# Low weight products one contraction block behind, and five queue orders fixed, in a hybrid conv/mLSTM decoder block

## The chip, the cores and the metric

The kernel runs on one core of one Trainium2 chip. The metric is the device time of one execution in microseconds (us). The kernel before takes 1734.45 us, the median of three runs (1732.58 to 1735.91).

The engines are called by their short names: PE (TensorE) does the matrix products and transposes, PEld loads its weights, DVE (VectorE) and ACT (ScalarE) work elementwise, POOL (GpSimd) does a little of that, and SP (SyncE) issues most of the DMA loads. Each engine works through its own queue in order; an instruction that waits holds up all that stands behind it on that engine.

## The reference

One block of a decoder on 1024 tokens with 1024 channels, in float32. Cut to what matters:

```python
h = rms_norm(x, norm_mix_g[l]) * (1.0 + sc1) + sh1
proj = jnp.einsum("bsd,de->bse", h, w_in[l]) + b_in[l]
glu_in, qk_in, v, o_pre, if_pre, merge_pre = jnp.split(proj, IN_SPLITS, axis=-1)
a = glu_in[..., :CONV_WIDTH] * jax.nn.sigmoid(glu_in[..., CONV_WIDTH:])
a = causal_depthwise_conv(a, conv_dw_w[l], conv_dw_b[l])          # 31 taps
qk = jax.nn.silu(causal_depthwise_conv(qk_in, qk_conv_w[l], qk_conv_b[l]))   # 4 taps
hm = mlstm_chunkwise(heads(q), heads(k) * (MLSTM_HEAD_DIM ** -0.5), heads(v), gates[...], gates[...])
y = jnp.einsum("bsd,de->bse", g_conv * y_conv + g_mlstm * y_mlstm, w_out[l])
x = x + g1 * y
h = rms_norm(x, norm_ffn_g[l]) * (1.0 + sc2) + sh2
gt, up = jnp.split(jnp.einsum("bsd,df->bsf", h, w_ffn_up[l]), 2, axis=-1)
x = x + g2 * jnp.einsum("bsf,fd->bsd", jax.nn.silu(gt) * up, w_ffn_down[l])
return rms_norm(x, final_norm_g)
```

The mLSTM has four heads of 256 channels; per chunk it forms decayed scores of q and k, multiplies them with v, and carries a state C from chunk to chunk. The feed-forward width is 2816.

## The kernel before

**Products in three parts.** Each float32 operand is split into a high part, rounded to the matmul's type (`hh`, `whi`), and a low part, the rest (`hl`, `wlo`). A product is the sum hi x hi + hi x lo + lo x hi. The high part of a weight is made by a copy on ACT (L148), the low part by a subtraction on DVE (L149). `mm_k` (L154) does one of eight contraction blocks of a 128 x 1024 output: for hi x hi, hi x lo and lo x hi in turn, two matmuls of 512 columns each, which accumulate in one PSUM tile `mm`. There are two such tiles. `block` and `wblock` run `mm_k` over the eight blocks, 48 matmuls in all.

**The order.** The program is written stage by stage, and a scheduler at build time decides the order in each engine's queue by priorities and what is free. `queue_behind(ins, earlier)` (L173) is a hand-made constraint: `ins` stands behind `earlier` in the queue of their engine. It adds no wait between engines.

**Stages.** Until 45 us conditioning and norm. To about 950 us: the GLU columns with the 31-tap convolution (DVE, L388), the projections and the four mLSTM heads, with projection blocks as other work for PE beside the chain of the chunks. Then w_out (L991 to L1010) and the second norm (to 1085), the up projection (`up_run`, to 1482), and the down projection in four groups of feed-forward blocks (to 1734).

**Heads.** For each head `qk_part` runs `qk_tile` four times, k, k, q, q: one `wblock`, an eviction with bias into `qkraw` (L530, ACT; one buffer), the first tap into `cacc` (L533, ACT; two buffers) and three more taps (L535, DVE). For k follow SiLU into `kf` and back into `cacc` (L539, L540), then `kh` (L543) and `kl` (L544). `v_part` makes v with its own weights in two halves (L583 on ACT, L584 on DVE) and 256-column matmuls (L601 to L605). `mlstm` (L647) goes over four chunks of 256 tokens: scores into `pa` (L627 to L629, in `three`), masking on DVE (L659, L660), their split `sch`, `scl` (L663, L664), transposes of `kf` (L674), scaled keys `kwh`, `kwl` (L676, L677), products with v into `pn` and with the state into `pc`, `num` (L697, L698), and for the first three chunks the new state `Cst` (L714), `Ch` (L715, ACT), `Cl` (L716, DVE). After two chunks `num` is normalised (L734) and transposed (L741). The `qk_part` of a head is written behind the `mlstm` of the head before; the scheduler draws it forward.

**Gate weights.** In `v_part` of head 0, L576 and L577 copy the weights of the gates into the tiles that also hold the v weights.

**Up projection.** `up_run` forms seven products per block of a fast 2 x 2 scheme (`product`, L1104, 12 matmuls each) into banks of PSUM: p1 and p5 share an `mm` tile, p2 and p7 the other, p6 is in `pa`, p3 in `pn`, p4 in `pc`. DVE adds combine them (L1136 to L1147).

**Down projection.** For each group and each of eight token blocks t: `act_split` (L1175) loads the activations and splits them (L1179 ACT, L1180 DVE), matmuls L1299 to L1301 sum into `mm`, and DVE adds the sum to x (L1303). For a block of the next group `down_raw` loads 512 KB of weights into `draw` (two buffers) and scales them on DVE (L1162), and `down_split` splits them into `fa` or `fb` (L1171, L1172).

## Time and profile before

| what | value |
|---|---|
| median of three runs | 1734.45 us (1732.58 to 1735.91) |
| the profiled execution | 1735.88 us |
| its span in the profile | 1734.1 us |
| busy, share of the span: DVE | 1249.7 us, 72% |
| busy, share of the span: ACT | 611.7 us, 35% |
| matmuls | 8360 |
| PE busy in 45 to 270 us | 223.49 of 225 us |
| in 270 to 305 us | 32.49 of 35 us |
| in 305 to 975 us | 667.70 of 670 us |
| in 975 to 1085 us | 103.27 of 110 us |
| in 1085 to 1482 us | 396.24 of 397 us |
| in 1482 to 1560 us | 75.96 of 78 us |

A row of the timeline gives start in us, duration in us, engine, line, operation, output <- inputs with their shapes, the number of instructions in a row that are joined in it, and in brackets the idle time before it and what ended that. A row of waits gives engine and line, what was waited for, total us, times, longest us. A row of windows gives the window, its length, then for PE, PEld, DVE, ACT and POOL busy us and instructions, the granted PE clock, the share of DMA time and GB/s.

### The profile page before, as it was taken

How to read it: one execution, taken by the hardware profiler on the slowest of the kernel's cores; microseconds unless marked ns; L12 is line 12 of the kernel's file. 1: busy time of each engine (PE TensorE's matmuls, PEld its weight loads, DVE VectorE, ACT ScalarE, POOL GpSimd, SP SyncE). 2: the span in 40 equal slices, each digit the busy share in tenths (PEclk: the TensorE clock that was granted, in tenths of full speed). 3: DMA queues.
4: the chain of work that ended last, by engine and by line, in shares of the span. 5: the costliest groups of instructions: out<-in, count | busy, mean ns of one | idle time of the engine just before them, and what ended most of it. 6: DMA issues, size and time to landing. Idle time of an engine off the chain costs nothing. (4 is left out here: it accounts for less than half of the span.)

```text
span 1734.1 us, 20875 instructions
## 1 busy us (share of the span) xinstructions
PE 1692.9 (98%) x8360; PEld 1418.6 (82%) x8360; DVE 1249.7 (72%) x1681; ACT 611.7 (35%) x809; POOL 52.7 (3%) x113
## 2 busy tenths in 40 slices
PE   5999999999999999999999998999999999999998
PEld 4788889888988888888888778888888888778887
DVE  6989998997799669446798668766666665685243
ACT  7424335323433253223522386322222222232122
POOL 0000001000001000000000000000000000000000
PEclk9999999999999999999999999999999999999999
DMA  9221120221111112243694743322222222653121
GB/s 320 63 62 49 37 71 28 61 73 49 37 49 61 61 49 61 73 146 98 209 376 167 230 152 104 98 86 85 86 73 75 84 81 96 226 168 101 58 94 52
DMA packets 194711, 179.91 MB, mean 104 GB/s; under 512 B 7463, under 2 KB 166711, under 8 KB 194615
## 3 DMA queue, kind: packets, MB, share of 16 engines
q1 hardware_dynamic: 177367, 146.61, 27.4%
q10 hardware_dynamic: 17248, 31.99, 5.0%
q8 instruction: 65, 1.06, 0.3%
q14 instruction: 31, 0.25, 0.0%
HBM read 146.06 MB, written 32.51 MB: 103 GB/s over the span
## 5 line engine op out<-in xcount | busy, mean ns | idle before, releaser
L388 DVE SCALAR_TENSOR_TENSOR cacc<-a,col,cacc 128x1024 f32<-128x1024 f32 x240 | 306.8, 1286 | 3.9 <-ACT cacc L386 1.4
L158 PE MATMUL mm<-hh,wlo 128*128 128x512 f32 x864 | 271.2, 391 | 1.5 <-DVE wlo L149 1.5
L158 PE MATMUL mm<-hl,whi 128*128 128x512 f32 x864 | 272.5, 392 | 0.0
L158 PE MATMUL mm<-hh,whi 128*128 128x512 f32 x864 | 271.6, 392 | 0.0
L158 PEld LDWEIGHTS mm<-hh,wlo 128*128 128x128 f32 x864 | 160.3, 188 | 33.6 <-DVE wlo L149 2.7
L158 PEld LDWEIGHTS mm<-hl,whi 128*128 128x128 f32 x864 | 161.0, 188 | 32.1 <-issue 0.5
L158 PEld LDWEIGHTS mm<-hh,whi 128*128 128x128 f32 x864 | 160.5, 188 | 31.6
L148 ACT ACTIVATE whi<-wraw 128x1024 fp32r<-128x1024 f32 x61 | 64.7, 1061 | 226.5 <-PE mm L158 171.3
L149 DVE TENSOR_TENSOR wlo<-wraw,whi 128x1024 fp32r<-128x1024 f32 x61 | 74.5, 1222 | 28.7 <-ACT whi L148 25.2
L1114 PE MATMUL mm<-Bh,gh 128*128 128x512 f32 (+1 forms) x192 | 71.5, 375 | 2.9 <-ACT gh L1051 1.5
L1115 PE MATMUL mm<-Bl,gh 128*128 128x512 f32 (+1 forms) x192 | 71.5, 373 | 0.6 <-DVE Bl L1033 0.6
L604 PE MATMUL mm<-wlo,hh 128*128 128x256 f32 x256 | 72.0, 282 | 0.0
L1116 PE MATMUL mm<-Bh,gl 128*128 128x512 f32 (+1 forms) x192 | 71.2, 371 | 0.0
L1303 DVE TENSOR_TENSOR x<-x,mm 128x1024 f32<-128x1024 f32 x24 | 29.3, 1219 | 52.0 <-PE mm L1301 49.6
L1179 ACT ACTIVATE whi<-wraw 128x512 fp32r<-128x512 f32 (+2 forms) x32 | 25.3, 792 | 114.8 <-PE mm L1301 75.8
L535 DVE SCALAR_TENSOR_TENSOR cacc<-qkraw,col,cacc 128x1024 f32<-128x1024 f32 x48 | 61.5, 1282 | 4.9 <-ACT cacc L533 4.5
L603 PE MATMUL mm<-whi,hh 128*128 128x256 f32 x192 | 54.6, 284 | 0.0
L605 PE MATMUL mm<-whi,hl 128*128 128x256 f32 x192 | 54.2, 283 | 0.0
L1299 PE MATMUL mm<-fa,whi 128*128 128x512 f32 x128 | 50.6, 396 | 1.6 <-DVE cu L1142 0.9
L1300 PE MATMUL mm<-fa,wlo 128*128 128x512 f32 x128 | 50.5, 395 | 1.2 <-DVE wlo L1180 1.2
L1301 PE MATMUL mm<-fa,whi 128*128 128x512 f32 x128 | 50.6, 395 | 0.0
L1052 DVE TENSOR_TENSOR ul<-uraw,uh 128x1024 fp32r<-128x1024 f32 x20 | 24.5, 1225 | 35.4 <-ACT uh L1051 35.4
(444 smaller groups left out, 3893.1 us busy)
## 6 DMA issues: line engine op xcount, KB each, us to landing
wraw<-in_w_in_dram SPq DMA_DIRECT2D x64, 512.0 KB
awt<-in_w_ada_dram SPq DMA_DIRECT2D x32, 512.0 KB
graw<-in_w_ffn_up_dram SPq DMA_DIRECT2D x24, 512.0 KB
uraw<-in_w_ffn_up_dram SPq DMA_DIRECT2D x22, 512.0 KB
draw<-in_w_ffn_down_dram SPq DMA_DIRECT2D x22, 512.0 KB
act_d<-cg ACTq DMA_DIRECT2D x38, 256.0 KB
wad<-in_w_ada_dram SPq DMA_DIRECT2D x16, 512.0 KB
wraw<-in_w_out_dram SPq DMA_DIRECT2D x16, 512.0 KB
```

Of the source, the lines that this page charges most:

```text
L148: nc.scalar.activation(hi, raw, AF.Copy)
L149: (eng or nc.vector).tensor_sub(lo, raw, hi.bitcast(F32))
L158: nc.tensor.matmul(flat(acc)[:, a:b], lhs[:, k, :], rhs[k][:, a:b], start=(first and k == 0), stop=(last and k == kt - 1))
L388: nc.vector.scalar_tensor_tensor(acc, a[:, j:j + S], dw_col(j, ct), acc, op0=OP.mult, op1=OP.add)
L535: nc.vector.scalar_tensor_tensor(cv, raw[:, j:j + S], wcol(j), cv, op0=OP.mult, op1=OP.add)
L603: nc.tensor.matmul(o, hh[k][:, ts_], his[k], start=False, stop=False)
L604: nc.tensor.matmul(o[:, 0:256], hh[k][:, ts_], los[k], start=False, stop=False)
L605: nc.tensor.matmul(o, hl[k][:, ts_], his[k], start=False, stop=(k == KT - 1))
L1114: nc.tensor.matmul(o, a, rh, start=(k == 0), stop=False)
L1115: nc.tensor.matmul(o, a, rl, start=False, stop=False)
L1116: nc.tensor.matmul(o, b, rh, start=False, stop=(k == 3))
L1299: nc.tensor.matmul(o, hi[:, i, :], his[i][:, a:b], start=(i == 0), stop=False)
```

## The change

1. `mm_k`: the lo x hi product of contraction block k is issued one block later, behind the high products of block k + 1; the last block issues its own too. The number of matmuls stays.
2. `qk_tile`: the three DVE taps (L535) are queued behind the last `Cl` subtraction that has been written so far, which is that of the third chunk of the head before.
3. `v_part`: the copies L576 and L577 get high priority.
4. `up_run`: for the last feed-forward block, product 3 is queued behind product 7, and product 4 behind product 3.
5. Down projection: the scaling of `draw` (L1162) is queued behind the addition to x (L1303) of the same t.
6. Down projection: `act_split` is issued one token block ahead.

```diff
--- before.py
+++ after.py
@@ -153,10 +153,15 @@
 
     def mm_k(acc, k, kt, w, xh, xl, parts=HALVES):
         hi, lo = w
-        for lhs, rhs, first, last in ((hi, xh, True, False), (hi, xl, False, False), (lo, xh, False, True)):
+        steps = [(hi, xh, k), (hi, xl, k)]
+        if k:
+            steps.append((lo, xh, k - 1))
+        if k == kt - 1:
+            steps.append((lo, xh, k))
+        for i, (lhs, rhs, j) in enumerate(steps):
             for a, b in parts:
-                nc.tensor.matmul(flat(acc)[:, a:b], lhs[:, k, :], rhs[k][:, a:b],
-                                 start=(first and k == 0), stop=(last and k == kt - 1))
+                nc.tensor.matmul(flat(acc)[:, a:b], lhs[:, j, :], rhs[j][:, a:b],
+                                 start=(k == 0 and i == 0), stop=(i == 3))
 
     def block(src, row0, kt, col0, xh, xl, w=None, busy=0):
         if w is None:
@@ -523,6 +528,8 @@
             nc.scalar.activation(t, t, AF.Exp, scale=sgn)
         nc.vector.tensor_scalar(wsc, wsc, 1.0 / 16, None, op0=OP.mult)
 
+    ahead = {}
+
     def qk_tile(col0, conv_i, scale, name):
         acc = yield from wblock(col0)
         raw = hp.tile([128, 3 + S], F32, name="qkraw", tag="qkraw")
@@ -532,7 +539,9 @@
         wcol = lambda j: cols["qk_w"][:, j * 16 + conv_i:j * 16 + conv_i + 1]
         nc.scalar.activation(cv, raw[:, 0:S], AF.Copy, scale=wcol(0))
         for j in range(1, 4):
-            nc.vector.scalar_tensor_tensor(cv, raw[:, j:j + S], wcol(j), cv, op0=OP.mult, op1=OP.add)
+            ins = nc.vector.scalar_tensor_tensor(cv, raw[:, j:j + S], wcol(j), cv, op0=OP.mult, op1=OP.add)
+            if "state" in ahead:
+                queue_behind(ins, ahead["state"])
         bias = cols["qk_b"][:, conv_i:conv_i + 1]
         if name == "k":
             kf = hp.tile([128, 768], F32, name=f"kf{conv_i % 2}")
@@ -573,8 +582,9 @@
             for i, t in enumerate(wide):
                 n = min(3, KT - 3 * i)
                 ks = slice(3 * i, 3 * i + n)
-                nc.vector.tensor_copy(t[:, 0:n, 256:264], wif_raw[:, ks])
-                nc.vector.tensor_sub(t[:, 0:n, 264:272], wif_raw[:, ks], t[:, 0:n, 256:264].bitcast(F32))
+                with tc.high_priority():
+                    nc.vector.tensor_copy(t[:, 0:n, 256:264], wif_raw[:, ks])
+                    nc.vector.tensor_sub(t[:, 0:n, 264:272], wif_raw[:, ks], t[:, 0:n, 256:264].bitcast(F32))
         for kh in range(2):
             raw, hi, lo = (wp.tile([128, KT, 128], dt, name=n, tag=n).rearrange("p (k a) e -> p k (a e)", a=2)
                            if n != "whi" or h else None for n, dt in (("wraw", F32), ("whi", F32R), ("wlo", F32R)))
@@ -713,7 +723,7 @@
                     else:
                         nc.vector.scalar_tensor_tensor(Cn[:, j, :], C[2][:, j, :], dec[:, c, h:h + 1], pc[:, 0:258], op0=OP.mult, op1=OP.add)
                     nc.scalar.activation(Ch[:, j, :], Cn[:, j, :], AF.Copy)
-                    nc.vector.tensor_sub(Cl[:, j, :], Cn[:, j, :], Ch[:, j, :].bitcast(F32))
+                    ahead["state"] = nc.vector.tensor_sub(Cl[:, j, :], Cn[:, j, :], Ch[:, j, :].bitcast(F32))
                 C = (Ch, Cl, Cn)
             if c % 2 == 0:
                 continue
@@ -1101,7 +1111,7 @@
     PART = {1: (0, 0, "B", 0), 2: (0, 4, "B", 1), 3: (2, 4, "D", 0), 4: (1, 4, "T", 3), 5: (1, 0, "T", 0),
             6: (2, 0, "T", 1), 7: (3, 0, "T", 2)}
 
-    def product(w, i, o, cs):
+    def product(w, i, o, cs, behind=None):
         wi, k0, kind, part = PART[i]
         hi, lo = w[wi]
         for k in range(4):
@@ -1111,9 +1121,12 @@
                 th, tl = (Bh, Bl) if kind == "B" else (Th, Tl)
                 rh, rl = th[k][:, part, cs], tl[k][:, part, cs]
             a, b = hi[:, k0 + k, :], lo[:, k0 + k, :]
-            nc.tensor.matmul(o, a, rh, start=(k == 0), stop=False)
+            begin = nc.tensor.matmul(o, a, rh, start=(k == 0), stop=False)
+            if k == 0 and behind:
+                queue_behind(begin, behind)
             nc.tensor.matmul(o, a, rl, start=False, stop=False)
-            nc.tensor.matmul(o, b, rh, start=False, stop=(k == 3))
+            end = nc.tensor.matmul(o, b, rh, start=False, stop=(k == 3))
+        return end
 
     def up_run(f, w, half=None):
         n = 512 if half is None else 256
@@ -1138,12 +1151,12 @@
         nc.vector.tensor_add(u2, s1, p[6])
         product(w, 5, p[5], cs)
         nc.vector.tensor_add(c12, u2, p[5])
-        product(w, 7, p[7], cs)
+        end = product(w, 7, p[7], cs)
         nc.vector.tensor_add(c21, u2, p[7])
         nc.vector.tensor_add(c22, c21, p[5])
-        product(w, 3, p[3], cs)
+        end = product(w, 3, p[3], cs, end if f == FT - 1 else None)
         nc.vector.tensor_add(c12, c12, p[3])
-        product(w, 4, p[4], cs)
+        product(w, 4, p[4], cs, end if f == FT - 1 else None)
         nc.vector.tensor_add(c21, c21, p[4])
         for i in range(2):
             nc.scalar.activation(cg[i], cg[i], AF.Silu)
@@ -1157,9 +1170,11 @@
 
     groups = [4, 4, 6, 8]
 
-    def down_raw(f, raw, row):
+    def down_raw(f, raw, row, earlier=None):
         nc.sync.dma_start(raw, wdn[f * 128:(f + 1) * 128, :])
-        nc.vector.tensor_mul(raw, raw, row)
+        ins = nc.vector.tensor_mul(raw, raw, row)
+        if earlier:
+            queue_behind(ins, earlier)
         return raw
 
     def down_split(gidx, i, raw):
@@ -1288,22 +1303,24 @@
         wd = []
         if gidx == 1:
             nc.sync.dma_start(grow, bass.AP(tensor=final_norm_g.tensor, offset=final_norm_g.offset, ap=[[0, 128], [1, D]]))
+        split = None
         for t in range(8):
-            hi, lo = act_split(f0, nf, t)
+            hi, lo = split or act_split(f0, nf, t)
             if gidx == 0:
                 x1.append(load_x1(t))
             if gidx < 3:
                 p = ps_mm()
+            split = act_split(f0, nf, t + 1) if t < 7 else None
             for o, a, b in (finish(t) if gidx == 3 else sums(flat(p))):
                 for i in range(nf):
                     nc.tensor.matmul(o, hi[:, i, :], his[i][:, a:b], start=(i == 0), stop=False)
                     nc.tensor.matmul(o, lo[:, i, :], his[i][:, a:b], start=False, stop=False)
                     nc.tensor.matmul(o, hi[:, i, :], los[i][:, a:b], start=False, stop=(i == nf - 1))
             if gidx < 3:
-                nc.vector.tensor_add(x1[t], x1[t], flat(p))
+                added = nc.vector.tensor_add(x1[t], x1[t], flat(p))
                 nn = groups[gidx + 1]
                 for i in range(len(wd), min(nn, (t + 1) * PACE)):
-                    wd.append(down_split(gidx + 1, i, down_raw(f0 + nf + i, fp.tile([128, D], F32, name="draw", tag="draw", bufs=2), g2row)))
+                    wd.append(down_split(gidx + 1, i, down_raw(f0 + nf + i, fp.tile([128, D], F32, name="draw", tag="draw", bufs=2), g2row, added)))
         f0 += nf
```

The lines of the changed kernel are shifted: by 5 from L158 on, by 7 at L530 to L535, by 9 or 10 in the rest of the heads and in w_out, by 13 to 17 in the down projection.

**DVE at the border of heads 0 and 1.** `cacc_2084` is the first k block of head 1, `cacc_2160` the second, `cacc_2237` the first q block, `wlo_2341` the second half of its v weights; `Cl_1849` is head 0's last state before the change and `Cl_1847` after. Before, from the second k block's taps on (those of `cacc_2084` stand 21 rows further ahead):

```order
L535 SCALAR_TENSOR_TENSOR cacc_2160<-qkraw_2157,col2_528,cacc_2160 128x1024 x2
L584 TENSOR_TENSOR wlo_2341<-wraw_2339,whi_2340 128x1024
L698 TENSOR_TENSOR num4_1772<-num4_1772,pn_1817 128x258
L535 SCALAR_TENSOR_TENSOR cacc_2160<-qkraw_2157,col2_528,cacc_2160 128x1024
L677 SCALAR_TENSOR_TENSOR kwl_1762<-pa_1763,wsc_691,kwh_1761 128x256
L699 BN_STATS st4_1773<-num4_1772 128x6
L700 BN_AGGR mv4_1774<-st4_1773 128x2
L714 SCALAR_TENSOR_TENSOR Cst_1498<-Cst_1498,dec_696,pc_1850 128x258
L714 SCALAR_TENSOR_TENSOR Cst_1498<-Cst_1498,dec_696,pc_1860 128x258
L716 TENSOR_TENSOR Cl_1849<-Cst_1498,Ch_1848 128x258
```

After, from the same state on:

```order
L669 TENSOR_TENSOR dms_1335<-dms_1335,pa_1868 128x256
L726 TENSOR_TENSOR Cl_1847<-Cst_1496,Ch_1846 128x258
L670 TENSOR_TENSOR dms_1335<-dms_1335,pa_1868 128x128
L542 SCALAR_TENSOR_TENSOR cacc_2084<-qkraw_2081,col2_528,cacc_2084 128x1024
L674 TENSOR_TENSOR scl_1884<-dms_1335,sch_1883 128x384
L542 SCALAR_TENSOR_TENSOR cacc_2084<-qkraw_2081,col2_528,cacc_2084 128x1024
L708 TENSOR_TENSOR num4_1770<-num4_1770,pn_1917 128x258
L542 SCALAR_TENSOR_TENSOR cacc_2084<-qkraw_2081,col2_528,cacc_2084 128x1024
```

Before, the taps of the second k block stand ahead of the second `kwl` and of the state. After, the taps of both k blocks and of the first q block stand behind the state, and so does `wlo_2341`, 22 rows further on, behind two taps of `cacc_2237`.

**PE at the same place.** `mm_2253` is the second q block of head 1, `mm_2345` its first v tile; `kf`, `kwl`, `sch`, `scl` belong to head 0's third and fourth chunk. Before, within the third chunk:

```order
L628 MATMUL pn_1789<-vl_702,sch_1735 128x258
L158 MATMUL mm_2253<-hh5_87,wlo_2250 128x512
L158 MATMUL mm_2253<-hh6_88,whi_2249 128x512 x2
L629 MATMUL pn_1789<-vh_701,scl_1736 128x258
L158 MATMUL mm_2253<-hl6_475,whi_2249 128x512 x2
L158 MATMUL mm_2253<-hh6_88,wlo_2250 128x512 x2
L158 MATMUL mm_2253<-hh7_89,whi_2249 128x512 x2
L158 MATMUL mm_2253<-hl7_476,whi_2249 128x512 x2
L158 MATMUL mm_2253<-hh7_89,wlo_2250 128x512 x2
L627 MATMUL pc_1850<-vh_701,kwh_1761 128x258
```

After, at the end of the fourth chunk:

```order
L637 MATMUL pn_1945<-vh_701,sch_1883 128x258
L638 MATMUL pn_1945<-vl_702,sch_1883 128x258
L639 MATMUL pn_1945<-vh_701,scl_1884 128x258
L163 MATMUL mm_2253<-hh0_82,whi_2249 128x512 x2
L163 MATMUL mm_2253<-hl0_308,whi_2249 128x512 x2
L163 MATMUL mm_2253<-hh1_83,whi_2249 128x512 x2
L163 MATMUL mm_2253<-hl1_309,whi_2249 128x512 x2
L163 MATMUL mm_2253<-hh0_82,wlo_2250 128x512 x2
```

Before, the q block's matmuls stand between those of the third chunk. After, all 48 stand behind the last score product of the fourth chunk, and the v tile behind them.

**SP in w_out.** `wraw_7753` is the fifth load of w_out, `graw` and `uraw` are the first weights of the up projection, `g1row` the row of gains. Before:

```order
L996 DMA wraw_7753<-in_w_out_dram 128x2x512
L945 DMA g1row_7600<-mrow_d0_7546 128x1024
L1047 DMA graw_7765<-in_w_ffn_up_dram 128x8x128
L1047 DMA uraw_7767<-in_w_ffn_up_dram 128x8x128
L996 DMA wraw_7804<-in_w_out_dram 128x2x512
L996 DMA wraw_7851<-in_w_out_dram 128x2x512
```

After:

```order
L955 DMA g1row_7600<-mrow_d0_7546 128x1024
L1057 DMA graw_7765<-in_w_ffn_up_dram 128x8x128
L1057 DMA uraw_7767<-in_w_ffn_up_dram 128x8x128
L1006 DMA wraw_7753<-in_w_out_dram 128x2x512
L1006 DMA wraw_7804<-in_w_out_dram 128x2x512
L1006 DMA wraw_7851<-in_w_out_dram 128x2x512
```

The load `wraw_7753` has moved from ahead of `g1row`, `graw_7765` and `uraw_7767` to behind them. No edit names it; it follows from the scheduler.

## The prediction

> **What bounds the kernel now.** I read the first part of the page, then TensorE's waits (the bound engine's), then the rows around each wait that the change touches, and the windows where the clock fell.
>
> ```profile
> PE 1692.9 (98%) x8360; PEld 1418.6 (82%) x8360; DVE 1249.7 (72%) x1681; ACT 611.7 (35%) x809; POOL 52.7 (3%) x113
> ```
>
> TensorE (PE) is busy for 1692.9 of 1734.1 us, and the change takes no matmul away. So time can only come from its idle time and from stretches at a lower clock, and any idle time that is added is paid in full. The rows of the waits that the edits touch (us in total, times, longest):
>
> ```profile
> PE pc L629 <- DVE kwl L677: 1.8, 1, 1.8
> PE mm L158 <- DVE wlo L149: 1.5, 2, 0.8
> PE pa L1003 <- ACT whi L997: 1.5, 1, 1.5
> ...
> PE mm L1300 <- DVE wlo L1180: 1.2, 1, 1.2
> ...
> PE mm L1299 <- DVE cu L1142: 0.9, 1, 0.9
> ...
> PE mm L1299 <- DVE x L1303: 0.8, 1, 0.8
> ...
> PE mm L603 <- DVE t L577: 0.6, 1, 0.6
> ```
>
> Without the L1003 row, which no edit aims at, they come to 6.8 us. Two of these waits are followed by a lower granted clock (first column the window, the last three the clock, the DMA share and GB/s):
>
> ```profile
> 270.00:273.00 3.00, 1.24 (x7) 1.03 (x8) 2.88 (x6) 1.00 (x2) 0.10 (x1) 0.91 0.42 92
> 273.00:276.00 3.00, 3.00 (x16) 3.00 (x16) 1.52 (x4) 2.97 (x6) 0.00 (x0) 0.52 0.27 82
> ...
> 1546.00:1550.00 4.00, 4.00 (x12) 3.14 (x12) 3.87 (x5) 2.64 (x3) 0.00 (x0) 0.62 0.40 135
> ```
>
> At clock 0.52 three us do the work of 1.56: 1.4 us lost, and 0.3 in the window before. The 4 us at 0.62 lose 1.5. So the kwl wait costs 1.8 + 1.7 = 3.5 us, with the 0.3 us wait for kwh just before it 3.8; the two waits in the down projection cost 1.2 + 0.8 + 1.5 = 3.5 us.
>
> **The change part by part.** *Low products one block behind (mm_k).* The rows around one of the two wlo waits:
>
> ```profile
> 483.17 0.40 PE L158 MATMUL mm<-hl,whi 128*128 128x512 f32 x1
> 484.31 0.74 PE L158 MATMUL mm<-hh,wlo 128*128 128x512 f32 x2 [0.74 <-DVE wlo L149]
> 484.89 0.40 PE L158 MATMUL mm<-hh,whi 128*128 128x512 f32 x1
> ...
> 262.62 0.62 PE L158 MATMUL mm<-hh,wlo 128*128 128x512 f32 x2
> 263.07 0.62 PE L158 MATMUL mm<-hh,whi 128*128 128x512 f32 x2
> ```
>
> Two matmuls take 0.45 us from start to start, so one takes 0.23. From 483.17 to 484.31 is 1.14 instead of 0.23, and the pair behind takes 0.58 instead of 0.45: 1.0 us lost, and as much at the other place. The first low product now stands behind eight matmuls instead of four: 4 x 0.23 = 0.9 us of cover against waits of 0.8 and 0.7. Both go: -2.0 us. Were the cover short by 0.2, the rest would still be waited for. The number of matmuls stays.
>
> *Copies of the gate weights at high priority.* VectorE's (DVE's) queue holds the same instructions in the same order up to well behind these copies, so the 0.6 us wait at L603 stays: 0.
>
> *Last up block.* The two products that now come last (p3 into pn, p4 into pc) are 24 matmuls, 5.5 us of cover behind p5 and p7, whose reading DVE adds made the first down matmul wait 0.9 us. That bank is free long before: -0.9 us.
>
> *Down projection.* What made x and wlo late (DVE):
>
> ```profile
> 1539.38 1.23 DVE L1162 TENSOR_TENSOR draw<-draw,g2row 128x1024 f32<-128x1024 f32 x1 [1.28 <-DMA draw<-in_w_ffn_down_dram]
> ...
> 1541.65 1.22 DVE L1303 TENSOR_TENSOR x<-x,mm 128x1024 f32<-128x1024 f32 x1
> 1542.79 1.22 DVE L1172 TENSOR_TENSOR fb<-draw,fb 128x1024 fp32r<-128x1024 f32 x1
> 1543.92 0.69 DVE L1180 TENSOR_TENSOR wlo<-wraw,whi 128x512 fp32r<-128x512 f32 x1
> ```
>
> DVE stood 1.3 us waiting for a draw load, with the add of x queued behind. Now the add goes first and the split of the next block is issued one block early. For a block of group 1 DVE has 1.2 + 1.2 + 0.7 + 1.2 = 4.3 us to do (from these rows), while TensorE computes 24 matmuls of 0.23 = 5.5 us. So both waits and their clock go: -3.5 us. What is queued behind the new wait (the scaling of draw behind the add) is fa or fb of the next group and the next wlo. In group 0 and at the border of groups 2 and 3 the sum comes close to 5.5 us: 0 to +1 us, I take +0.5.
>
> *Heads.* This is the large term. Before, the four-tap convolution of the first k block of head 1 ran during head 0's second chunk, so the next block could be evicted early:
>
> ```profile
> 237.71 1.29 DVE L535 SCALAR_TENSOR_TENSOR cacc<-qkraw,col,cacc 128x1024 f32<-128x1024 f32 x1
> ...
> 242.22 1.10 ACT L530 ACTIVATE qkraw<-mm,col 128x1024 f32<-128x1024 f32 x1
> ```
>
> That freed a PSUM bank for the last q block, and its 48 matmuls and the v part filled TensorE's waits in head 0's last two chunks. Now these taps stand behind head 0's last state. TensorE's queue after the change has no block matmul between the k transposes of the third chunk and the last score product of the fourth; the q block comes behind them. Its bank waits for a chain with these steps (DVE, then ScalarE, ACT):
>
> ```profile
> 260.43 0.56 DVE L664 TENSOR_TENSOR scl<-dms,sch 128x384 fp32r<-128x384 f32 x1
> ...
> 271.88 0.48 DVE L677 SCALAR_TENSOR_TENSOR kwl<-pa,wsc,kwh 128x256 fp32r<-128x256 f32 x1
> ...
> 276.12 0.28 DVE L660 TENSOR_TENSOR dms<-dms,pa 128x128 f32<-128x128 f32 x1
> ...
> 279.52 2.60 DVE L535 SCALAR_TENSOR_TENSOR cacc<-qkraw,col,cacc 128x1024 f32<-128x1024 f32 x2
> 282.05 0.42 DVE L698 TENSOR_TENSOR num<-num,pn 128x258 f32<-128x258 f32 x1
> ...
> 269.22 1.22 DVE L584 TENSOR_TENSOR wlo<-wraw,whi 128x1024 fp32r<-128x1024 f32 x1
> ```
>
> ```profile
> 272.00 0.94 ACT L539 ACTIVATE kf<-cacc,col 128x768 f32<-128x768 f32 x1 [2.14 <-DVE cacc L535]
> 272.84 0.49 ACT L540 ACTIVATE cacc<-cacc,col 128x256 f32<-128x256 f32 x1
> 273.24 1.10 ACT L530 ACTIVATE qkraw<-mm,col 128x1024 f32<-128x1024 f32 x1
> ...
> 276.04 0.83 ACT L543 ACTIVATE kh<-kf 128x768 fp32r<-128x768 f32 x1
> 276.78 0.40 ACT L543 ACTIVATE kh<-cacc 128x256 fp32r<-128x256 f32 x1
> ...
> 278.03 1.16 ACT L533 ACTIVATE cacc<-qkraw,col 128x1024 f32<-128x1024 f32 x1 [0.44 <-DVE kl L544]
> ```
>
> From the end of Cl: dms 0.3, three taps of 1.3 with scl 0.6 and num 0.4 between them, kf 0.9 and 0.5, qkraw 1.1: 7.7 us, some 7.1 where one step overlaps the next (two taps show 2.60 and the next row begins 0.07 before their end). Until then TensorE has 4 state and 9 value products left, at 0.12 each (half of a 512-column matmul) 1.6 us. It waits 5.5 us. Ahead of Cl, where nothing fills either, the wlo copy queued before the first kwl (1.2) and a kwl step (0.5) are seen as waits, 1.7 us.
>
> Behind the q block the v part needs, after its first 13 matmuls, the second half of its own weights, and their wlo is now queued behind all taps of the second k block and two taps of the q block. Counted from the bank's release: kh 1.2, cacc 1.2, three taps 3.9, kf and qkraw 2.5, kh 1.2, cacc 1.2, two taps 2.6, wlo 1.2, together 15.0 us; TensorE has 48 x 0.23 + 13 x 0.12 = 12.6 us of work. That is a wait of 2.4 us. It is smaller by what a lower clock stretches the q block, and larger by DVE's normalisation of head 0, which stands in the same queue: 0 to 4 us, I take 2.4.
>
> For the clock I take what this place lost before, 1.7 us after waits of 0.3 and 1.8 us, once for the long wait and once for the v part's: 3.4 us.
>
> Heads: 1.7 + 5.5 + 2.4 + 3.4 = 13.0 us in place of 3.8, so **+9.2 us**. The low end is the long wait alone with no loss of clock, 5.5 - 3.8 = +1.7; the high end has the v part at 4, +10.8. I take the middle sum, since the queues are fixed and every step has a row. Between the later heads the taps stood behind the state already, nearly all of them, and blocks remain as filler: 0.
>
> The trace speaks here on how short a wait lowers the clock: 1.8 us with 0.3 before it. The Trainium skill ("TensorE: Matmul & The Clock Gate", Part 1: The HAM clock gate) puts it at idle gaps of about 3.4 us. The trace does not agree: 0.52 was granted after the shorter wait. By the page the short waits would cost no clock, before or after: the two removed places would be worth 1.7 and 1.5 us less and the v part's wait 1.7 us less, which makes the total 1.5 us larger.
>
> *A load that moves by the way (w_out).* SyncE's queue now has the fifth w_out load behind three others (queue, then its users):
>
> ```profile
> 953.95 0.40 SPq L996 DMA_DIRECT2D wraw<-in_w_out_dram  x1
> ...
> 957.31 1.09 SPq L1047 DMA_DIRECT2D uraw<-in_w_ffn_up_dram  x1
> ```
>
> ```profile
> 961.91 1.06 ACT L997 ACTIVATE whi<-wraw 128x1024 fp32r<-128x1024 f32 x1 [2.89 <-PE mm L1004]
> ...
> 973.38 1.06 ACT L997 ACTIVATE whi<-wraw 128x1024 fp32r<-128x1024 f32 x1 [0.85 <-DMA wraw<-in_w_out_dram]
> ```
>
> ```profile
> 972.04 0.69 DVE L1060 TENSOR_TENSOR s<-graw,uraw 128x512 f32<-128x512 f32 x1 [0.32 <-DMA uraw<-in_w_ffn_up_dram]
> ```
>
> ```profile
> 967.38 0.39 PE L1003 MATMUL pa<-whi,y 128*128 128x512 f32 x1
> ```
>
> It was issued at 953.95 and is now issued behind uraw, after 958.4. TensorE uses it from 967.38. If it lands with uraw (972.0), whi is there at 973.1 and TensorE waits 5.7 us, of which the 1.5 us wait for the next whi is given back: +4.2. If it lands by 966.3: 0. I take +2.5, above the middle, since uraw stands straight ahead of it and landed late.
>
> *Sum:* -2.0 - 0.9 - 3.5 + 0.5 + 9.2 + 2.5 = **+5.8 us**. The profiled execution took 1735.88 us (span 1734.1 and 1.8 around it), so it would take 1741.7. It lies 1.4 us above the median of 1734.45, and against that median the forecast is **1740.3 us**.
>
> **The rivals.** 0.2%, about what a measurement can tell from no change here, is 3.5 us.
>
> *The gains arrive and the heads cost little (faster).* The chain behind Cl costs no more than the 3.8 us lost there before, because DVE comes to the state early (three taps fewer ahead of it) and the v part's weights are ready, and w_out's load lands in time. Then -2.0 - 0.9 - 3.5 = -6.4: 1728.0 us. For it: DVE has these 3.9 us less ahead. Against it: the taps start at Cl, however early that is, and TensorE has 1.6 us to do. It decides where the idle time behind Cl falls under 1.5 us. Chance 0.2.
>
> *Only the long wait (no change).* v part and w_out find cover, and the clock is lost once: 5.5 + 1.7 - 3.8 = +3.4, less 6.4, plus 0.5: -2.5 us, 1732 us; with w_out's load half late, 1734.5 us. The v part's chain has 2.4 us of excess only if each step starts at once, so this is near. Chance 0.22.
>
> *The change doesn't do what it says.* Only for the gate copies, priced at 0 already.
>
> *The forecast:* the heads pay the whole chain, 0.58.
>
> **The range.** The low ends of heads (+1.7), down and w_out (0) with -6.4 give 1729.7; the high ends (+10.8, +1, +4.2) give +9.6, 1744.1, and the runs spread by 1.5 us on top: 1729.7 to 1745.6. The forecast's own cases reach from 1737.9 to 1745.6. Faster by over 0.2% has 0.2, within it 0.22, slower 0.58.
>
> **What would show it.** Right: in the changed profile no wait for wlo at mm_k's blocks, none for cu or x at the first down products, and clock 1.0 in the down projection; between head 0's last Cl and the q block TensorE waits for qkraw (L530, now L537) some 5 us, then for the v part's wlo some 2 us, with a clock near 0.5 after each. Wrong: if the block matmuls fill that place although queued behind, or a wait there stays under 2 us, the heads' term falls and with it the sign. The w_out term is wrong if TensorE waits less than 1.5 us in all for whi there.

## The result and the profile after

The changed kernel takes 1738.35 us (median of nine runs, 1738.1 to 1741.4) against 1734.45 (nine runs, 1732.58 to 1737.22): the ratio is 1.0028, 95% interval 1.0018 to 1.0037, or 3.1 to 6.4 us slower. Its profiled execution took 1738.27 us (span 1736.5), which is its median; that of before, 1735.88 (span 1734.1), was 1.4 us above its own. So the two traces differ by only 2.4 us, and the medians by 3.9.

TensorE's waits after the change, first those of the places that the change was to close or that the prediction named:

```profile
PE mm L163 <- ACT qkraw L537: 2.6, 1, 2.6
PE pa L1013 <- ACT whi L1007: 2.4, 1, 2.4
...
PE pn L637 <- DVE num L708: 1.9, 2, 1.1
...
PE mm L1015 <- DVE wlo L1008: 1.5, 1, 1.5
...
PE mm L1124 <- DVE cg L1148: 1.0, 1, 1.0
...
PE mm L613 <- DVE t L587: 0.6, 1, 0.6
PE pn L639 <- DVE scl L674: 0.5, 1, 0.5
PE mm L1124 <- DVE cu L1155: 0.5, 1, 0.5
PE pc L637 <- ACT kwh L686: 0.5, 2, 0.3
```

The waits for kwl, for wlo in `mm_k`, and for cu, x and wlo at the down products are gone. In their place stand four at the heads, a longer one at w_out, and two in the up projection (L1124). The wait at the gate copies (L613) has stayed at 0.6.

Where the time went is read from the start of matmuls with the same number in TensorE's queue (counted from zero), in places where both kernels run the same work there (us, after less before, from the two traces; the right column is the difference over the stretch):

| matmul, start before | after less before | stretch |
|---|---|---|
| 300th, 84.2 | -0.1 | |
| 1500th, 300.3 | +6.7 | border of heads 0 and 1: +6.8 |
| 3000th, 583.5 | +4.6 | the two places of wlo: -2.1 |
| 4800th, 942.5 | +4.5 | -0.1 |
| 5700th, 1114.9 | +5.6 | w_out and second norm: +1.1 |
| 7200th, 1462.5 | +5.6 | 0 |
| first down product, 1482.1 | +6.6 | last up block: +1.0 |
| last, 1727.8 | +2.4 | down projection: -4.2 |

The heads, DVE first, then ACT, then the clock. In the DVE rows the taps L542 begin as soon as Cl and dms are done:

```profile
263.59 0.42 DVE L726 TENSOR_TENSOR Cl<-Cst,Ch 128x258 fp32r<-128x258 f32 x1
263.93 0.28 DVE L670 TENSOR_TENSOR dms<-dms,pa 128x128 f32<-128x128 f32 x1
264.12 1.28 DVE L542 SCALAR_TENSOR_TENSOR cacc<-qkraw,col,cacc 128x1024 f32<-128x1024 f32 x1
265.32 0.55 DVE L674 TENSOR_TENSOR scl<-dms,sch 128x384 fp32r<-128x384 f32 x1
265.79 1.28 DVE L542 SCALAR_TENSOR_TENSOR cacc<-qkraw,col,cacc 128x1024 f32<-128x1024 f32 x1
266.98 0.42 DVE L708 TENSOR_TENSOR num<-num,pn 128x258 f32<-128x258 f32 x1
267.32 1.28 DVE L542 SCALAR_TENSOR_TENSOR cacc<-qkraw,col,cacc 128x1024 f32<-128x1024 f32 x1
```

```profile
268.63 0.94 ACT L548 ACTIVATE kf<-cacc,col 128x768 f32<-128x768 f32 x1 [1.78 <-DVE cacc L542]
269.47 0.49 ACT L549 ACTIVATE cacc<-cacc,col 128x256 f32<-128x256 f32 x1
269.87 1.09 ACT L537 ACTIVATE qkraw<-mm,col 128x1024 f32<-128x1024 f32 x1
```

```profile
264.00:267.00 3.00, 1.69 (x9) 1.02 (x7) 3.00 (x6) 2.54 (x4) 0.00 (x0) 1.00 0.00 0
267.00:270.00 3.00, 0.99 (x6) 0.78 (x6) 2.98 (x10) 1.37 (x3) 0.36 (x4) 0.97 0.00 0
270.00:273.00 3.00, 1.98 (x5) 1.60 (x6) 1.45 (x4) 3.00 (x4) 2.14 (x5) 0.50 0.00 0
273.00:276.00 3.00, 3.00 (x9) 2.32 (x8) 2.96 (x7) 0.04 (x1) 0.00 (x0) 0.50 0.00 0
276.00:279.00 3.00, 3.00 (x14) 2.43 (x13) 2.12 (x2) 0.81 (x1) 0.10 (x1) 0.89 0.00 0
...
1540.00:1550.00 10.00, 10.00 (x46) 8.28 (x45) 7.49 (x9) 3.39 (x4) 0.00 (x0) 1.00 0.43 131
```

From the end of Cl (264.01) to the eviction's end (270.96) the chain takes 6.95 us, and the q block starts at 271.02. DVE is busy almost throughout from 264 to 270, then ACT until 271, and TensorE is not; then the q block runs its first 5.6 us, to 276.67, at half clock. In the down projection, last row, the clock is 1.00 where it had been 0.62.

The load of w_out (ACT, then TensorE): the conversion stood 9.4 us waiting for its load, and TensorE for the conversion.

```profile
973.23 1.06 ACT L1007 ACTIVATE whi<-wraw 128x1024 fp32r<-128x1024 f32 x1 [9.41 <-DMA wraw<-in_w_out_dram]
```

```profile
974.34 0.50 PE L1013 MATMUL pa<-whi,y 128*128 128x512 f32 x1 [2.40 <-ACT whi L1007]
```

### The profile page after: what moved, and what is told of

The parts are those of the page before. It is cut to its first block, busy times and chain, and to the rows that moved or that the text cites. A ratio compares the mean times of both kernels' runs of the same rounds, so it can differ in the third digit from the quotient of the medians.

```text
span 1736.5 us, 20860 instructions
## 1 busy us (share of the span) xinstructions
PE 1694.9 (98%) x8360; PEld 1420.9 (82%) x8360; DVE 1250.8 (72%) x1681; ACT 611.6 (35%) x809; POOL 54.4 (3%) x113
## 5 line engine op out<-in xcount | busy, mean ns | idle before, releaser
L163 PE MATMUL mm<-hh,wlo 128*128 128x512 f32 x864 | 263.0, 392 | 0.0
L1124 PE MATMUL mm<-Bh,gh 128*128 128x512 f32 (+1 forms) x192 | 71.5, 375 | 2.0 <-ACT gh L1061 1.4
L542 DVE SCALAR_TENSOR_TENSOR cacc<-qkraw,col,cacc 128x1024 f32<-128x1024 f32 x48 | 61.5, 1281 | 7.5 <-ACT cacc L540 6.7
L613 PE MATMUL mm<-whi,hh 128*128 128x256 f32 x192 | 54.3, 284 | 0.0
```

The source lines that it names most:

```text
L163: nc.tensor.matmul(flat(acc)[:, a:b], lhs[:, j, :], rhs[j][:, a:b], start=(k == 0 and i == 0), stop=(i == 3))
L542: ins = nc.vector.scalar_tensor_tensor(cv, raw[:, j:j + S], wcol(j), cv, op0=OP.mult, op1=OP.add)
L1124: begin = nc.tensor.matmul(o, a, rh, start=(k == 0), stop=False)
```

## The experiments

Each kernel ran in several rounds against the kernel before on the same chip; ratios are to that kernel, with 95% intervals. Stretches are measured as in the table above.

**Each edit taken out.** The taps are free again:

```diff
-            ins = nc.vector.scalar_tensor_tensor(cv, raw[:, j:j + S], wcol(j), cv, op0=OP.mult, op1=OP.add)
-            if "state" in ahead:
-                queue_behind(ins, ahead["state"])
+            nc.vector.scalar_tensor_tensor(cv, raw[:, j:j + S], wcol(j), cv, op0=OP.mult, op1=OP.add)
```

> The changed kernel without edit 2 (the taps of q and k are not queued behind the state). Theory A (one buffer qkraw, so late taps hold back the q block, and its 48 matmuls no longer fill the chain of head 0): the traces put the border of heads 0 and 1 at +6.6 us, so 1738.35 - 6.6 = 1731.7 us; the waits for num, scl and qkraw and the clock of 0.50 at 258 to 276 us go, and the wait for kwl (1.8) with its clock comes back. Rival B (the time lies in the load of w_out and in later stages, the head's waits are only moved there): 1736 us or more.

Measured: 1729.76 us, ratio 0.9974 (0.9963 to 0.9986). By the trace the head stretch is 1.9 us faster than before instead of 6.8 slower, so with the other edits in place this one costs 8.7 us there. Its waits at the heads:

```profile
PE pc L637 <- DVE kwl L685: 1.1, 1, 1.1
PE pc L635 <- ACT kwh L684: 0.3, 1, 0.3
```

The kwl wait came back at 1.1, not 1.8, and without a fall of the clock. Theory A holds, and was 2 us too small. The wait for wlo at 304 us also came back (0.9), which the taps behind the state had moved away.

The last up block is ordered by the scheduler again:

```diff
-        product(w, 3, p[3], cs, end if f == FT - 1 else None)
+        product(w, 3, p[3], cs)
-        product(w, 4, p[4], cs, end if f == FT - 1 else None)
+        product(w, 4, p[4], cs)
```

> The changed kernel without edit 4 (the scheduler orders the last up block again). Theory A (products 3 and 4 were the work that filled the waits between products 2 and 7; put last, they uncover 0.5 and 1.0 us and close 0.9): the place costs 0.9 us less, 1737.4 us, with a wait for cu of about 0.9 at the first down product and none for cg. Rival B (the two new waits come from the down edits, which queue other work on VectorE there): both stay and the 0.9 comes on top, 1739.3 us.

Measured: 1737.82 us, ratio 1.0017 (1.0008 to 1.0026): against the 1.0028 of the changed kernel the intervals overlap, so the time alone settles nothing. The trace does. From product 1 of the block ahead of the last (1450.5 us before, 1456.1 after) to the first down product it takes 31.6 us, as before, where the changed kernel takes 32.6. (The expectation for edit 4 alone, further down, names product 1 of the last block; its 31.6 and 32.6 are counted from the block ahead too.) The waits from there on:

```profile
PE mm L1316 <- DVE cu L1155: 0.9, 1, 0.9
PE mm L1316 <- DVE x L1320: 0.5, 1, 0.5
```

No wait for cg: theory A. A wait for x of 0.5 came in the down projection, which gives back part. (The profiled execution, at 1741.08 us the slowest of its eleven, also lost 2.9 us more than the changed kernel in the second norm, where it waited 3.2 us for gh instead of 1.4.)

The low products in their own block again (the body of `mm_k` as before):

> The changed kernel without edit 1 (the low products in their own contraction block). Theory A: the two waits for wlo come back at 0.9 to 1.06 each, +2.0 us, and the fifth load of w_out is issued ahead of the three others again, -1.1 us (974 to 1010 us): 1739.2 us. Rival B (the w_out stage is limited by its loads as a whole, their order does not matter): +2.0, 1740.4 us, with the waits at w_out as in the changed kernel (2.4 and 1.5).

Measured: 1739.83 us, ratio 1.0029 (1.0019 to 1.004). One wlo wait came back (0.7 at 491 us); the other, at 305 us, did not, as the taps' order has moved it. The load of w_out went ahead of the three others again, and the stretch from 940 to 1110 us was 1.6 us faster than before instead of 1.1 slower. So theory A holds for the load and for one of the two waits; the other is closed by edit 2, with edit 1 or without it.

The down projection without its two edits:

```diff
-g2row, added)))
+g2row)))
-            hi, lo = split or act_split(f0, nf, t)
+            hi, lo = act_split(f0, nf, t)
-            split = act_split(f0, nf, t + 1) if t < 7 else None
```

> The changed kernel without edits 5 and 6 (scaling of draw not behind the add, activations not split ahead). Theory A: the down projection loses 4.1 us again with waits for x and wlo and a clock of about 0.6 behind them: 1742.4 us. Rival B (that the waits went because the stage starts later and its loads had arrived): 1738 to 1739 us without such waits.

Measured: 1741.4 us, ratio 1.0038 (1.0025 to 1.005). From the first down product to the last it takes 244.9 us, against 241.8 with the edits and 246.0 before:

```profile
PE mm L1316 <- DVE wlo L1195: 2.3, 2, 1.2
```

So 3.1 of the 4.2 us are the edits' and 1.1 us came without them. Theory A, with B's share in it. Over all traces the stage takes 241.8 to 242.7 us in the nine with these two edits and 243.5 to 246.0 in the five without; the kernel before is the slowest of them, so 4.2 is the upper end of what they are worth.

**Without edits 2 and 4** (both diffs above):

> The changed kernel without edits 2 and 4 (edits 1, 3, 5 and 6 stay). Theory A (the places add up): the border of the heads at -2 against before as in the run with the taps free, the last up block 1.0 less than in the changed kernel, of which 0.5 may come back as a wait for x in the down projection: 1729.76 - 0.5 to 1.0 = 1728.8 to 1729.3 us. Rival B (the gains are not additive, another stage takes them back): 1730 us or more.

Measured: 1729.33 us, ratio 0.9973 (0.9964 to 0.9982), which is within the noise of the run without edit 2 alone; the up block is 31.6 us again, and 0.6 of the 1.0 us came back as a longer down projection (242.4). Theory A on the whole.

**The place of the load.** Beside the two edits taken out (f = 0 are the first loads of graw and uraw):

```diff
-            nc.sync.dma_start(raw, wo[kk * 256:(kk + 1) * 256, es].rearrange("(k p) e -> p k e", p=128))
+            wo_load[q, eh, kk] = nc.sync.dma_start(raw, wo[kk * 256:(kk + 1) * 256, es].rearrange("(k p) e -> p k e", p=128))
...
+        if f == 0:
+            queue_behind(ins, wo_load[0, 1, 0])
```

> As the run without edits 2 and 4, with the first load of graw queued behind the fifth load of w_out. Theory A (the fifth load's place in the queue sets the wait for whi there): that wait is 1.5 us or less instead of 2.4, the stage from 940 to 1110 us about 1.0 us shorter, 1728 us. Rival B (the loads of that stage take as long in either order): no difference, 1729 us, a wait of 2.4 again there or 1 us more behind it.

Measured: **1725.42 us, ratio 0.9951 (0.9937 to 0.9964)**, faster than both kernels. The conversions of the fifth and the sixth load:

```profile
959.64 1.06 ACT L1006 ACTIVATE whi<-wraw 128x1024 fp32r<-128x1024 f32 x1 [3.52 <-DMA wraw<-in_w_out_dram]
...
967.41 1.06 ACT L1006 ACTIVATE whi<-wraw 128x1024 fp32r<-128x1024 f32 x1 [2.72 <-DMA wraw<-in_w_out_dram]
```

They start at 959.6 and 967.4, where in the run without this edit they start at 966.0 and 970.3, and before at 961.9 and 973.4 (with TensorE 2.8 us later). No wait of TensorE is left in w_out, and the stretch is 4.1 us shorter than in the run without this edit: four times what A expected. That run waited 2.5 us for whi there, and behind the wait its clock was halved, which cost 1.7 us more:

```profile
968.17:971.59 3.42, 3.42 (x10) 0.50 0.47 158
```

The edit moved more than the fifth load: the sixth was issued at 957.4 instead of 962.1, so the 4.1 us belong to the new order of both, which is not the order before either. The same edit on the changed kernel with all its edits:

> The changed kernel with all its edits, and the first load of graw queued behind the fifth load of w_out. Theory A (the place of that load alone costs the time of the stage): the border of the heads stays at +6.7, the stage from 940 to 1110 us takes 4 to 5 us less than in the changed kernel and has no wait for whi over 0.5: 1733.0 to 1734.3 us. Rival B (TensorE is later there by the heads' loss, so the loads have had their time already): at most the wait of 2.4 goes, 1736 us.

Measured: 1735.54 us, ratio 1.0002 (0.9994 to 1.0011). The stretch takes 4.0 us less than in the changed kernel (2.9 less than before instead of 1.1 more), the heads still lose 7.0. Theory A for the stretch; the total is 1.2 to 2.5 us longer than it said, with 0.6 us of it a wait for modc at 881 us and 0.3 at the heads, where the v part's wait for wlo was 1.4.

**Edit 2 alone, and edit 2 without the first block.**

> The kernel before with edit 2 alone (taps behind the state). Theory A (the edit alone makes the loss at the heads): the waits for num, scl and qkraw appear, the clock falls to 0.5 for some 6 us, +6.6 to 8.6 us: 1741.4 to 1743.4 us. Rival B (it needs the low products' new order, which lets the scheduler place the blocks otherwise): under +3 us, 1737 us or less.

Measured: 1742.3 us, ratio 1.004 (1.0027 to 1.0052). The waits at the heads:

```profile
PE pn L631 <- DVE num L702: 2.3, 2, 1.2
PE mm L158 <- ACT qkraw L532: 1.9, 1, 1.9
PE mm L608 <- DVE wlo L588: 1.3, 1, 1.3
PE pc L631 <- ACT kwh L680: 0.7, 2, 0.4
PE pn L633 <- DVE scl L668: 0.5, 1, 0.5
```

The stretch is 7.4 us longer than before. Theory A. The trace as a whole is only 3.5 us longer, 3 us under this kernel's median, since the w_out and second norm stretch is 2.0 us shorter in it and the down projection 2.5. L608 is the v part's wait for its second weights, which the changed kernel only just missed.

```diff
-            if "state" in ahead:
+            if "state" in ahead and conv_i != 10 and conv_i != 12 and conv_i != 14:
```

> As the run without edits 2 and 4, but with edit 2 for all blocks except the first k block of a head. Theory A (a block's late taps hold qkraw and with it the PSUM bank of the next block, whichever block it is): the q block's matmuls fill the third chunk again, and the v part waits for its bank behind the state, some 5 us by the same chain, so +4 to +7 us against that run: 1733 to 1736 us. Rival B (only the first block's taps matter, the others stood almost behind the state before): within 1 us of it, 1728 to 1730 us.

Measured: 1736.41 us, ratio 1.0013 (1.0004 to 1.0021), 7.1 us above the run without edits 2 and 4. Theory A, at the upper end: the q block fills the third chunk, no wait for kwl is left, and the idle time stands behind the state, at the v part, whose bank the next eviction frees:

```profile
276.66 0.39 PE L639 MATMUL pn<-vh,scl 128*128 128x258 f32 x1 [1.26 <-DVE scl L674]
278.19 0.58 PE L637 MATMUL pn<-vh,sch 128*128 128x258 f32 x1 [1.14 <-DVE num L708]
281.76 0.58 PE L611 MATMUL mm<-vb_two,ones_v 128*128 128x256 f32 x1 [1.91 <-ACT qkraw L537]
```

**Edits alone on the kernel before.** The down projection's two:

> The kernel before with edits 5 and 6 alone. Theory A (the order of VectorE's queue made x and wlo late): from the first down product to the last 4 us less than before, no wait for x or wlo over 0.3 us, clock 1.0: 1730.3 us. Rival B (the waits come from the instant at which the stage meets its loads, as the run with edit 2 alone lost 2.5 us less there without these edits): 1732 us, with a wait for wlo left.

Measured: 1732.56 us, ratio 0.9981 (0.9972 to 0.9989). The down projection takes 242.3 us instead of 246.0 (-3.7), with no wait for x or wlo over 0.3: theory A by the waits, though the time alone would fit B. The total is 2.3 us above A's number; 1.6 us of that are in the second norm, which waited 2.8 us for gh (1.5 before). At the heads nothing was changed, and yet this run was 1.2 us faster there than before. TensorE's rows and the clock, here and in the run with edit 4 alone (whose heads are unchanged too), show why:

```profile
272.46 0.51 PE L631 MATMUL pc<-vh,kwl 128*128 128x258 f32 x2 [1.77 <-DVE kwl L679]
```

```profile
270.00:273.00 3.00, 1.23 (x8) 1.00 0.36 92
273.00:276.00 3.00, 2.97 (x25) 1.00 0.28 83
```

```profile
272.37 0.73 PE L631 MATMUL pc<-vh,kwl 128*128 128x258 f32 x2 [1.77 <-DVE kwl L679]
```

```profile
270.00:273.00 3.00, 1.23 (x7) 0.91 0.38 93
273.00:276.00 3.00, 3.00 (x16) 0.52 0.27 82
```

The same wait of 1.77 us leaves the clock at 1.00 in the first and takes it to 0.52 in the second. The traces also hold the instants at which the clock changes. It is either 1.00 or 0.50, and in each of the fourteen traces these instants lie whole multiples of 3.41 us apart. Cut at this step (counted back from a change at 1043.11 us in the first trace, and at a change itself, 272.48, in the second), the two places read:

```profile
268.28:271.69 3.41, 2.10 (x16) 1.00 0.02 5
271.69:275.11 3.42, 2.62 (x19) 1.00 0.53 149
```

```profile
269.06:272.48 3.42, 1.34 (x10) 1.00 0.18 35
272.48:275.89 3.41, 3.41 (x17) 0.50 0.40 119
```

In the first the cut falls into the wait, and TensorE is busy for over 2 us on either side. In the second the whole wait lies in one window, with the 0.31 us for kwh ahead of it; TensorE is busy for 1.34 us of that window, and the next one runs at half clock.

The low products' order alone:

> The kernel before with edit 1 alone. Theory A (it closes the waits for wlo and by its shift the clock's fall behind kwl; it also moves the fifth load of w_out): -2.9 us up to 940 us, -0.5 to +1.1 us from there to 1110 us, -1.8 to -3.4 us in all: 1731.0 to 1732.6 us. Rival B (only the two waits close): -2.0 and +1.1, 1733.5 us.

Measured: 1731.61 us, ratio 0.9981 (0.9972 to 0.999). That is within theory A's bounds: -2.7 us up to 940 us and no change from there to 1110 us by the trace. But only one of the two waits for wlo is closed; the one at 305 us is still there, with 0.9 us at 304.4.

The up block's order alone:

> The kernel before with edit 4 alone. Theory A (as the run with the up block free says): from the last block's product 1 to the first down product 32.6 us instead of 31.6, waits of 0.5 for cu and 1.0 for cg, none of 0.9 at the first down product: +1.0 us, 1735.4 us, less what the down projection gives back. Rival B (those two waits need the other edits): -0.9 us, 1733.5 us.

Measured: 1735.95 us, ratio 1.0006 (0.9997 to 1.0015), unclear as a time. The trace has 32.6 us, from the block ahead to the first down product, and the waits of theory A, 1.0 for cg and 0.5 for cu.

## Why the prediction was right

The forecast was 1740.3 us, +5.8; measured was +3.9 by the medians and +4.9 by the ratio. The sign and the main cause were right; one term had the wrong sign. That the total came within 2 us is in part luck: by the traces the heads, w_out and the down projection came out 1.2 to 2.4 us lower than forecast and the last up block 1.9 us higher, and the low products reached their number by the help of another edit.

- **Heads: +9.2 forecast, +6.8 in the trace, 8.7 by taking the edit out, 7.4 by doing it alone.** The chain behind Cl was worked out at 7.1 us and took 6.95. The sizes inside differ: 1.3 us of waits ahead of Cl (1.7 forecast: 0.2 and 0.3 for kwh, 0.8 for num), 4.3 behind it (5.5: 0.55, 1.15, 2.57), 0.2 at the v part (2.4). The clock fell once, from 269.8 to 276.7 us, and not twice; on the q block that cost 2.8 us (3.4 forecast for two falls). These come to 8.6 us against 13.0 forecast. About 2 us more (0.5 before) went into slow first matmuls behind the waits, an estimate from the starts of the matmuls against 0.23 and 0.12 us in dense rows; the sum left these out. TensorE came to the v part as its wlo was done, because the q block before it ran at half clock: that loss and the wait take each other's place, as the prediction said in passing, but the sum then counted both. The traces with this order show the exchange: the half clock reaches 5.6 us into the q block in the changed kernel, with no wait for the v part's wlo, 4.5 us without the down edits, with a wait of 0.6, and 2.9 us with the load moved, with a wait of 1.4.

  That the loss comes by way of the bank, and not from the taps' own time on DVE, is seen in the run with the first block free, where the idle time moved to the next user of a bank; no run gave `qkraw` a second buffer, which would test it directly. The low rival (+1.7 to +3.4) is refuted.
- **Low products: -2.0 forecast, -2.1 in the trace, but only half of it is this edit's.** Both waits went. The one at 484 us goes with edit 1 and comes back without it. The one at 305 us goes with edit 2, also in the two runs with edit 2 that leave edit 1 out, and stays at 0.9 with edit 1 alone: there TensorE comes 1.9 us sooner and DVE makes this wlo only 0.7 us sooner (303.1 instead of 303.8), so the 0.9 us of cover are used up. So "both go" failed for the edit by itself, and the sum came out by the help of another. The 2.7 us that edit 1 gives alone up to 940 us are 0.8 behind 300 us and 1.9 at the heads, where the wait for kwl falls from 1.8 to 1.1 us and the clock stays at 1.00; that gain was not forecast, and the taps' order hides it in the changed kernel.
- **Gate copies: 0.** The wait stayed at 0.6.
- **Last up block: -0.9 forecast, +1.0 measured, with and without the other edits.** This step failed. The wait at the first down product did go, by the cover worked out. But the 24 matmuls of the last block's p3 and p4 had been cover elsewhere: in the queue before, ten of them stood in the middle of the block ahead (behind its product 2), twelve ahead of the last block's product 1, two behind its product 2. Without them product 1 waits 0.5 us until the block ahead has been read (cu), and product 7 waits 1.0 for the add into cg, which reads product 2 from the PSUM tile that both share. DVE comes late to cg, because the scalings of draw begin only behind the adds of the block ahead:

```profile
1473.20 3.49 DVE L1175 TENSOR_TENSOR draw<-draw,g2row 128x1024 f32<-128x1024 f32 x3
...
1477.20 1.22 DVE L1175 TENSOR_TENSOR draw<-draw,g2row 128x1024 f32<-128x1024 f32 x1
1478.34 1.22 DVE L1187 TENSOR_TENSOR fa<-draw,fa 128x1024 fp32r<-128x1024 f32 x1
1479.47 0.68 DVE L1148 TENSOR_TENSOR cg<-su,mm 128x512 f32<-128x512 f32 x1
```

  Before, they ran from 1467.6 to 1472.3 and cg at 1475.3. I priced the place to which the work was moved and not the one from which it was taken.
- **Down projection: -3.5 + 0.5 forecast, -4.2 in the trace.** By taking the edits out 3.1, alone 3.7, so 4.2 is at the upper end; the feared waits in group 0 and at the border of groups 2 and 3 did not come. The lost clock was in it.
- **w_out: +2.5 forecast, +1.1 in the trace.** The load's new place goes with edit 1: it is there in the nine runs with this edit, two of which move it back by hand, and in none without. In the other seven TensorE takes 0.9 to 1.4 us longer than before from 942 us to the 5220th matmul, near the end of w_out (1036.9 us before). To 1115 us they spread from -0.5 to +4.0, but that comes behind w_out, in the second norm, where TensorE waits 0.9 to 3.2 us for gh. The conversion was expected at the latest on uraw's landing at 972.0 us, whi at 973.1; it started at 973.2, so the load landed past the bound. The wait was 2.4 and not 5.7. That TensorE was 4.5 us later by then is not why: with the taps free it is 3.0 us earlier than before, and the wait is 2.4 too, since the load is issued earlier as well (950.8 instead of 958.3). Seen from TensorE the issue stands where it stood before (953.8 in the time of the kernel before, 953.95 there), and not 4.4 us later as the prediction took it; what moved is the landing, 15 us behind the issue. The prediction also did not see that the order before was poor: with graw behind the load, 4.1 us go.
- **Profile against median.** I took the profiled execution's 1.4 us above the median as an offset that stays. Its trace holds 1.7 us of lost clock at the kwl wait, which the same kernel need not have: the run with the down edits alone had the same wait without it. That would make the 1.4, but it is not shown: the run with edit 4 alone lost the same clock there, and its profiled execution was 0.6 us under its median.

On the clock, the prediction set the trace against the Trainium skill ("TensorE: Matmul & The Clock Gate", Part 1, "What's actually happening"). The same section says that the window of the gate runs freely and is not reset by the kernel. The two runs with the same 1.77 us wait and clocks of 1.00 and 0.52 agree with that: what a short wait costs depends on when it comes. So do the instants at which the clock changes, always whole steps of 3.41 us apart. The prediction's alternative, by which short waits cost no clock and the total is 1.5 us larger, does not hold here: waits of 0.31 and 1.77 us that fell into one such window halved the clock, as the prediction had read from the first trace.

## What to carry to other kernels

When an order is fixed so that one engine's wait goes, look first for who holds a buffer until the delayed instruction has run: here three taps of 1.3 us held one buffer, that held a PSUM bank, and the bank held the only work that filled a dependent chain. Work that is moved to cover one wait uncovers another, so the place it leaves is priced like the place it goes to. And a scheduler may move loads that no edit names; here that order was worth 4 us, more than most of the edits.

## What was not expected of the hardware

What a short wait costs in clock depended on where it fell between fixed instants. From 60 us to the last matmul, every stretch at half clock in the fourteen traces lasts one, two or three steps of 3.41 us. Of the windows of that length that began at full clock, 19 were followed by half clock, and TensorE was busy for 9 to 60% of them; all the others, in which it was busy for 52% or more, were not. So an idle time of 1.77 us at the same place halved the clock in one run and left it at 1.00 in another, for 1.2 us of difference in the stretch. After the long wait of the changed kernel the clock stayed at 0.50 for two windows, from 269.84 to 276.67 us, 5.6 us into dense matmuls that began at 271.0.
